# Row variances on one core: the first two loads move ahead of the end of the tile context, everything else behind it

## The chip, the core and the metric

The kernel runs on one core of a Trainium2 chip. The core has five engines with an instruction stream each: TensorE (PE, not used here for computing), VectorE (DVE), ScalarE (ACT), GpSimd (POOL) and SyncE (SP), which here only issues DMA transfers. They meet through semaphores: an instruction can wait until a semaphore has a value and can change one when it is done. Data come from HBM into the core's on-chip memory (SBUF, 128 partitions) over 16 DMA engines. The metric is the device time of one execution in microseconds; the times shown are medians of several.

## The reference

```
def setup_inputs():
    batch, seq, dim = 32, 512, 1024
    return {
        "x": np.random.randn(batch, seq, dim).astype(np.float32),
    }

def reference(x: np.ndarray) -> np.ndarray:
    mean_sq = np.mean(x**2, axis=-1)
    sq_mean = np.mean(x, axis=-1)**2
    return (mean_sq - sq_mean).astype(np.float32)
```

So each of 32 x 512 = 16,384 rows of 1,024 numbers gives one number, its variance. 67.1 MB are read and 64 KB written.

## The kernel before

**Tiling.** The 16,384 rows are spread over 128 partitions, so each partition has 128 rows, called columns here. One column is a tile of 128 x 1,024 numbers. Columns 0 to 95 go through two buffers, `xt0` and `xt1`, of 16 columns (8.4 MB) each, in three turns of two groups (`TURNS`, `NBUF`, `GROUP`). Columns 96 to 127 are the end: loads of 8 and 8 columns back into `xt0`, then 5, 4, 2, 2, 1 and 1 columns and two halves of the last column into `xt_end`, 10 loads in all.

**Who computes.** Of the 16 columns of a group ACT takes six (`NACT`), in batches of three: a pass that sums (`act_mean`, L117), then a pass that squares around the mean and sums (`act_var`, L122). DVE takes ten: two statistics instructions of 512 numbers for each (`halves`, L113) and one that joins them (L216). POOL copies finished variances from `stage` to `mv` (L165) and joins the statistics of eleven end columns (L173 to L192). At the end `END_WHO` says which column is whose; column 126 is ACT's, the halves of column 127 are DVE's.

**Order.** The order of each engine's instructions is written by hand, and so are all waits. SP issues the first two loads at once; the load that refills a buffer waits for `done`, which DVE steps when a group is finished; then the 10 loads of the end; then three stores: columns 0 to 15, the columns up to 120, and the last seven. The last store waits for the last instructions of ACT and DVE (L303, L304). Each load steps its own semaphore (`landed`, `landed_end`) by 16, one for each DMA engine; the stores step `stored`.

**The context.** Tiles and semaphores come from the pools of a tile context (`tc`), and the whole body lies in one `tile_critical` block (L144). What the context adds is no line of the kernel, but it is in the built program: at the entry POOL runs a NOP that steps a semaphore, and every other engine that computes or issues waits for it in a branch; behind the body the engines run a drain each (L144), POOL gathers their semaphores, SP gathers them too, and then come a barrier over all five engines, two instructions of POOL that clear ranges of semaphores, and a second barrier (L308, the end of the context). A barrier here is a drain on each engine, a count that POOL waits for, and a release that POOL gives. Behind all that SP waits until `stored` is 48, that is, until the three stores have landed, and clears that semaphore (L309, L310). One more barrier stands ahead of the body (L325), behind four small constants that POOL writes.

**Place of the code.** Ahead of the body, ACT and DVE each have an alignment (L142): the next instruction of that engine is placed 128 instructions behind a boundary of `FETCH_BLOCK_INSTRUCTIONS`. The loader fills with instructions that are jumped over.

Of the kernel before, what the change touches and what calls it, by code (L numbers as in the profile page):

```python
# [11 lines left out]
def kernel(  # L12
# [14 lines left out]
    nc = tc.nc  # L27
    P = nc.NUM_PARTITIONS
# [6 lines left out]
    N, D = xf.shape  # L35
# [23 lines left out]
    pool = ctx.enter_context(tc.tile_pool(name="pool", bufs=1))  # L59
    xt = [pool.tile([P, GROUP, D], FP32, name=f"xt{b}") for b in range(NBUF)]  # L60
    xt_end = pool.tile([P, ncols - END0 - FIRST, D], FP32, name="xt_end")
    mv = pool.tile([P, 2, ncols], FP32, name="mv")
    stage = pool.tile([P, PER_TURN, 2], FP32, name="stage")
    stats = pool.tile([P, PER_TURN, 2, 6], FP32, name="stats")
    stats_join = pool.tile([P, JOINED, 2, 6], FP32, name="stats_join")
    stats_end = pool.tile([P, ncols - END0, 4, 6], FP32, name="stats_end")
    neg_mean = pool.tile([P, PER_TURN], FP32, name="neg_mean")
    neg_mean_end = pool.tile([P, ncols - END0], FP32, name="neg_mean_end")
    two = pool.tile([P, JOINED, 2], FP32, name="two")
    mu = pool.tile([P, JOINED, 1], FP32, name="mu")  # L70
    dev = pool.tile([P, JOINED, 4], FP32, name="dev")
    psum = ctx.enter_context(tc.tile_pool(name="psum", bufs=1, space=bass.MemoryType.PSUM))
    junk = [pool.tile([P, D], mybir.dt.bfloat16, name=f"junk{i}") for i in range(ACT_BATCH)]
    junk_sq = [psum.tile([P, D], FP32, name=f"junk_sq{i}") for i in range(ACT_BATCH)]

    sync, act, dve, gps = nc.sync, nc.scalar, nc.vector, nc.gpsimd
    landed = [tc.alloc_semaphore(f"landed{b}") for b in range(NBUF)]
    NEND = len(END_LOADS) + len(PIECES)
    landed_end = [tc.alloc_semaphore(f"landed_end{b}") for b in range(NEND)]
    go = tc.alloc_semaphore("go")  # L80
    act_done = tc.alloc_semaphore("act_done")
    done = tc.alloc_semaphore("done")
    copied = tc.alloc_semaphore("copied")
    dve_step = tc.alloc_semaphore("dve_step")
    act_step = tc.alloc_semaphore("act_step")
    gps_step = tc.alloc_semaphore("gps_step")
    stored = nc.alloc_semaphore("stored")

    def load(dst, c0, n, sem, f0=0, f=D):
        b0, pitch, row0 = next(b for b in BLOCKS if b[0] <= c0 < b[0] + b[1])  # L90
        assert c0 + n <= b0 + pitch
        ap = [[pitch * D, P], [D, n], [1, f]] if n > 1 else [[pitch * D, P], [1, f]]
        sync.dma_start(  # L93
            out=dst,
            in_=dataclasses.replace(xf, offset=(row0 + c0 - b0) * D + f0, ap=ap),
        ).then_inc(sem, 16)
# [47 lines left out]
    with tc.tile_critical(sync_engine=ENG.Pool, no_gpsimd_drain=True):  # L144

        for g in range(TURNS * NBUF):
            if g >= NBUF:
                sync.wait_ge(done, g - NBUF + 1)
            load(xt[g % NBUF], g * GROUP, GROUP, landed[g % NBUF])
        sync.wait_ge(done, (TURNS - 1) * NBUF + 1)  # L150
        c = END0
        for b, n in enumerate(END_LOADS):
            k = c - END0
            buf, k = (xt[0], k) if k < FIRST else (xt_end, k - FIRST)
            load(buf[:, k : k + n, :] if n > 1 else buf[:, k, :], c, n, landed_end[b])
            c += n
        f = 0
        for b, n in enumerate(PIECES, len(END_LOADS)):
            load(end_col(c)[:, f : f + n], c, 1, landed_end[b], f, n)
            f += n  # L160

        gps.sem_inc(copied, 1)
        for t in range(TURNS):
            gps.wait_ge(done, (t + 1) * NBUF)
            gps.tensor_copy(  # L165
                out=mv[:, 1, t * PER_TURN : (t + 1) * PER_TURN], in_=stage[:, :, 1]
            ).then_inc(copied, 1)

        part = stats_join.rearrange("p n h (e s) -> p n (h e) s", s=3)
        mean, m2 = part[:, :, :, 1], part[:, :, :, 2]  # L170
        gps.wait_ge(dve_step, 1)
        steps = [
            lambda: gps.tensor_tensor(out=two, in0=mean[:, :, 0:2], in1=mean[:, :, 2:4], op=ALU.add),  # L173
            lambda: gps.tensor_tensor(out=mu, in0=two[:, :, 0:1], in1=two[:, :, 1:2], op=ALU.add),
            lambda: gps.tensor_scalar(out=mu, in0=mu, scalar1=0.25, scalar2=None, op0=ALU.mult),
            lambda: gps.tensor_tensor(out=dev, in0=mean, in1=mu.to_broadcast([P, JOINED, 4]), op=ALU.subtract),
            lambda: gps.tensor_tensor(out=dev, in0=dev, in1=dev, op=ALU.mult),
            lambda: gps.tensor_scalar(out=dev, in0=dev, scalar1=D / 4.0, scalar2=None, op0=ALU.mult),  # L178
            lambda: gps.tensor_tensor(out=dev, in0=dev, in1=m2, op=ALU.add),
            lambda: gps.tensor_tensor(out=two, in0=dev[:, :, 0:2], in1=dev[:, :, 2:4], op=ALU.add),  # L180
            lambda: gps.tensor_tensor(out=mu, in0=two[:, :, 0:1], in1=two[:, :, 1:2], op=ALU.add),
        ]
        k = 0
        runs = []
        for j, c in enumerate(joined):
            if runs and runs[-1][1] + runs[-1][2] == c:
                runs[-1][2] += 1
            else:
                runs.append([j, c, 1])
        for j, c, n in runs:  # L190
            steps.append(
                lambda j=j, c=c, n=n: gps.tensor_scalar(  # L192
                    out=mv[:, 1, c : c + n], in0=mu[:, j : j + n, 0],
                    scalar1=1.0 / D, scalar2=None, op0=ALU.mult,
                )
            )
        for k, step in enumerate(steps):
            if k:
                gps.wait_ge(gps_step, k)
            step().then_inc(gps_step, 1)  # L200
        gps_steps = len(steps)

        with nc.Fori(0, TURNS, engines=[ENG.DVE]):
            take(dve, copied, 1)
            for b in range(NBUF):
                take(dve, landed[b], 16)
                dve.sem_inc(go, 1)
                mine = range(b * GROUP + NACT, (b + 1) * GROUP)
                for j in mine:
                    last = halves(stats[:, j, :, :], xt[b][:, j - b * GROUP, :])  # L210
                last.then_inc(dve_step, 1)
                take(dve, dve_step, 1)
                for j in mine:
                    if j == mine[-1]:
                        take(dve, act_done, 1)
                    last = dve.bn_aggr(out=stage[:, j, :], in_=stats[:, j, :, :])  # L216
                last.then_inc(done, 1)
        n = 0
        waiting = None
        seen = -1  # L220
        for b, c, who in end_cols:
            if who != "D":
                continue
            if b != seen:
                dve.wait_ge(landed_end[b], 16)
                seen = b
            col = end_col(c)
            if c in joined:
                last = halves(stats_join[:, joined.index(c), :, :], col)
                if c == joined[-1]:  # L230
                    last.then_inc(dve_step, 1)
                    n += 1
                continue
            st = stats_end[:, c - END0, :2, :]
            dve.bn_stats(out=st[:, 0, :], in_=col[:, :H])  # L235
            if waiting:
                waiting()
            n += 1
            dve.bn_stats(out=st[:, 1, :], in_=col[:, H:]).then_inc(dve_step, 1)  # L239
            dve_step_of.setdefault(b, n)  # L240

            def waiting(n=n, c=c, st=st):
                dve.wait_ge(dve_step, n)
                return dve.bn_aggr(out=mv[:, :, c], in_=st)  # L244

        c = ncols - 1
        st = stats_end[:, c - END0, : len(PIECES), :]
        f = 0
        for i, size in enumerate(PIECES):
            dve.wait_ge(landed_end[len(END_LOADS) + i], 16)  # L250
            last = dve.bn_stats(out=st[:, i, :], in_=end_col(c)[:, f : f + size])  # L251
            if i == 0:
                waiting()
            f += size
        n += 1
        last.then_inc(dve_step, 1)
        dve.wait_ge(dve_step, n)
        dve.bn_aggr(out=mv[:, :, c], in_=st).then_inc(dve_step, 1)
        dve_steps = n + 1

        act.preload_act_table(ACTF.Square)  # L261
# [15 lines left out]
        for b in range(len(END_LOADS)):  # L277
            mine = [c for bb, c, who in end_cols if bb == b and who == "A"]
            if not mine:
                continue  # L280
# [60 lines left out]
```

## Time and profile before

| what | value |
|---|---|
| time, median of 3 runs | 163.78 us (163.43 to 163.83) |
| time of the profiled execution | 163.64 us |
| its span | 161.9 us |
| what lies around the span | 1.74 us |
| DVE busy | 103.7 us (64%) |
| ACT busy | 106.3 us (66%) |
| POOL busy | 3.6 us (2%) |
| DMA, mean over the span | 415 GB/s |
| first load issued, first group started by DVE | 0.87 us, 23.11 us |
| last ACT pass ends | 160.0 us |

The span runs from the first instruction of the program to the end of its last one, as the profiler recorded them. The time is larger, since it holds work at the start and at the end that belongs to no line of the program. Places in the trace are microseconds from the span's start. Engines are named as above, with a "q" where the instruction is one that only the engine's sequencer runs (waits, drains, branches, DMA issues); those aren't counted as busy. A group of instructions is named by its line in the kernel, its operation, what it writes and reads, and how often it occurs.

### The profile page before, as it was taken

How to read it: one execution, taken by the hardware profiler on the slowest of the kernel's cores; microseconds unless marked ns; L12 is line 12 of the kernel's file. 1: busy time of each engine (PE TensorE's matmuls, PEld its weight loads, DVE VectorE, ACT ScalarE, POOL GpSimd, SP SyncE). 2: the span in 40 equal slices, each digit the busy share in tenths (PEclk: the TensorE clock that was granted, in tenths of full speed). 3: DMA queues.
4: the chain of work that ended last, by engine and by line, in shares of the span. 5: the costliest groups of instructions: out<-in, count | busy, mean ns of one | idle time of the engine just before them, and what ended most of it. 6: DMA issues, size and time to landing. Idle time of an engine off the chain costs nothing. (4 is left out here: it accounts for less than half of the span.)

```text
span 161.9 us, 579 instructions
## 1 busy us (share of the span) xinstructions
DVE 103.7 (64%) x232; ACT 106.3 (66%) x189; POOL 3.6 (2%) x18
## 2 busy tenths in 40 slices
DVE  0000029980599607994099921999039979999994
ACT  3000029990599807996099941999139999799985
POOL 0000000000000000000000000000000000005100
DMA  7969979989988998998997997997989999999991
GB/s 263 518 275 502 518 324 453 518 356 421 518 389 389 518 405 372 518 421 356 518 437 340 518 437 340 518 470 308 518 348 429 421 470 405 400 434 411 423 394 27
DMA packets 2738, 67.19 MB, mean 415 GB/s; under 512 B 688, under 2 KB 688, under 8 KB 1200
## 3 DMA queue, kind: packets, MB, share of 16 engines
q1 hardware_dynamic: 2736, 67.18, 96.7%
q14 instruction: 2, 0.02, 0.1%
HBM read 67.11 MB, written 0.07 MB: 415 GB/s over the span
## 5 line engine op out<-in xcount | busy, mean ns | idle before, releaser
L113 DVE BATCH_NORM_STATS2 stats<-xt 128x6 f32<-128x512 f32 x120 | 71.8, 678 | 49.9 <-DVEq L109 49.9
L117 ACT ACTIVATE junk<-xt 128x1024 bf16<-128x1024 f32 x41 | 42.7, 1042 | 50.4 <-ACTq L109 49.3
L122 ACT ACTIVATE junk_sq<-xt,neg_mean 128x1024 f32<-128x1024 f32 x36 | 39.7, 1104 | 1.5
L113 DVE BATCH_NORM_STATS2 stats_join<-xt 128x6 f32<-128x512 f32 x22 | 13.2, 677 | 0.0
L216 DVE BATCH_NORM_AGGREGATE stage<-stats 128x2 f32<-128x12 f32 x60 | 6.0, 166 | 6.2 <-DVEq L109 5.3
L117 ACT ACTIVATION_READ_ACCUMULATOR junk<-xt 128x1 f32 x41 | 7.6, 186 | 0.0
L122 ACT ACTIVATE junk_sq<-xt_end,neg_mean_end 128x1024 f32<-128x1024 f32 x6 | 6.7, 1111 | 0.1
L122 ACT ACTIVATION_READ_ACCUMULATOR junk_sq<-xt,neg_mean 128x1 f32 x36 | 6.7, 186 | 0.0
L117 ACT ACTIVATE junk<-xt_end 128x1024 bf16<-128x1024 f32 x6 | 6.3, 1046 | 0.4 <-DMA xt_end<-in_x_dram 0.2
L235 DVE BATCH_NORM_STATS2 stats_end<-xt_end 128x6 f32<-128x512 f32 x9 | 6.1, 675 | 0.0
L239 DVE BATCH_NORM_STATS2 stats_end<-xt_end 128x6 f32<-128x512 f32 x9 | 5.8, 642 | 0.0
L122 ACT ACTIVATE junk_sq<-xt,neg_mean_end 128x1024 f32<-128x1024 f32 x5 | 5.5, 1106 | 0.1
L165 POOL COPY mv<-stage 128x32 f32<-128x32 f32 x3 | 0.6, 210 | 133.0 <-DVE stage L216 133.0
L261 ACT ACT_TABLE_LOAD x1 | 1.3, 1283 | 1.3 <-PEq L325 1.3
L244 DVE BATCH_NORM_AGGREGATE mv<-stats_end 128x2 f32<-128x12 f32 x9 | 1.7, 191 | 0.0
L251 DVE BATCH_NORM_STATS2 stats_end<-xt_end 128x6 f32<-128x512 f32 x2 | 1.3, 668 | 0.1
L117 ACT ACTIVATION_READ_ACCUMULATOR junk<-xt_end 128x1 f32 x6 | 1.1, 188 | 0.0
L122 ACT ACTIVATION_READ_ACCUMULATOR junk_sq<-xt_end,neg_mean_end 128x1 f32 x6 | 1.1, 186 | 0.0
L122 ACT ACTIVATION_READ_ACCUMULATOR junk_sq<-xt,neg_mean_end 128x1 f32 x5 | 0.9, 188 | 0.0
L173 POOL TENSOR_TENSOR two<-stats_join 128x22 f32<-128x22 f32 x1 | 0.3, 252 | 12.9 <-DVE stats_join L113 12.9
L192 POOL TENSOR_SCALAR mv<-mu 128x6 f32<-128x6 f32 (+1 forms) x2 | 0.5, 236 | 0.2
L178 POOL TENSOR_SCALAR dev<-dev 128x44 f32<-128x44 f32 x1 | 0.3, 331 | 0.1
(12 smaller groups left out, 2.3 us busy)
## 6 DMA issues: line engine op xcount, KB each, us to landing
xt<-in_x_dram SPq DMA_DIRECT2D x2, 4096.0 KB, 19.5
xt_end<-in_x_dram SPq DMA_DIRECT2D x1, 2560.0 KB, 29.8
xt_end<-in_x_dram SPq DMA_DIRECT2D x1, 2048.0 KB, 34.2
xt_end<-in_x_dram SPq DMA_DIRECT2D x2, 1024.0 KB, 37.1
xt_end<-in_x_dram SPq DMA_DIRECT2D x2, 512.0 KB, 39.3
xt_end<-in_x_dram SPq DMA_DIRECT2D x2, 256.0 KB, 40.0
xt<-in_x_dram SPq DMA_DIRECT2D x6, 24.5
out_dram<-mv SPq DMA_DIRECT2D x1, 52.5 KB, 4.4
```

The costliest lines, as they stand in the source:

```text
L113: last = dve.bn_stats(out=st[:, h, :], in_=xcol[:, h * H : (h + 1) * H])
L117: return act.activation(out=junk[i], in_=xcol, func=ACTF.Copy, scale=-S / D, accum_out=nm)
L122: return act.activation(out=junk_sq[i], in_=xcol, func=ACTF.Square, scale=S, bias=nm, accum_out=var)
L165: gps.tensor_copy(out=mv[:, 1, t * PER_TURN : (t + 1) * PER_TURN], in_=stage[:, :, 1]).then_inc(copied, 1)
L173: lambda: gps.tensor_tensor(out=two, in0=mean[:, :, 0:2], in1=mean[:, :, 2:4], op=ALU.add),
L192: lambda j=j, c=c, n=n: gps.tensor_scalar(out=mv[:, 1, c : c + n], in0=mu[:, j : j + n, 0], scalar1=1.0 / D, scalar2=None, op0=ALU.mult,)
L216: last = dve.bn_aggr(out=stage[:, j, :], in_=stats[:, j, :, :])
L235: dve.bn_stats(out=st[:, 0, :], in_=col[:, :H])
L239: dve.bn_stats(out=st[:, 1, :], in_=col[:, H:]).then_inc(dve_step, 1)
L244: return dve.bn_aggr(out=mv[:, :, c], in_=st)
L251: last = dve.bn_stats(out=st[:, i, :], in_=end_col(c)[:, f : f + size])
L261: act.preload_act_table(ACTF.Square)
```

## The change

Tiles and semaphores no longer come from the context's pools but from the core's own allocators. The `tile_critical` block is gone. Inside the context only three things are left: the two alignments and the first two loads, whose semaphores the context is told not to handle. Then the context is closed, and all else, word for word as it was but one level further out, is written behind it. At the end SP clears the kernel's own semaphores, from `landed0` to `gps_step`, behind the issue of the last store, and then waits for `stored` as before.

In the built program the entry NOP of POOL and the branches that wait for it are gone, and so are the drains, gathers, POOL's two clears and the two barriers behind the body. Two barriers over all five engines, with one more drain on SP, now stand between the first two loads and the rest. DVE's and ACT's instructions are the same in the same order; on both, the four instructions of those two barriers now lie between the alignment and the body.

```
-    pool = ctx.enter_context(tc.tile_pool(name="pool", bufs=1))
-    xt = [pool.tile([P, GROUP, D], FP32, name=f"xt{b}") for b in range(NBUF)]
...
+    def sbuf(name, shape, dtype):
+        return nc.alloc_sbuf_tensor(name, shape, dtype).ap()
+
+    def psum(name, shape, dtype):
+        return nc.alloc_psum_tensor(name, shape, dtype).ap()
+
+    xt = [sbuf(f"xt{b}", [P, GROUP, D], FP32) for b in range(NBUF)]
...
-    landed = [tc.alloc_semaphore(f"landed{b}") for b in range(NBUF)]
+    landed = [nc.alloc_semaphore(f"landed{b}") for b in range(NBUF)]
...
     stored = nc.alloc_semaphore("stored")
+    sems = [*landed, *landed_end, go, act_done, done, copied, dve_step, act_step, gps_step]
...
-        sync.dma_start(
+        return sync.dma_start(
...
     for engine in (act, dve):
         engine.addr_align(FETCH_BLOCK_INSTRUCTIONS, offset=HEAD, max_nops=0)
 
-    with tc.tile_critical(sync_engine=ENG.Pool, no_gpsimd_drain=True):
-
-        for g in range(TURNS * NBUF):
-            if g >= NBUF:
-                sync.wait_ge(done, g - NBUF + 1)
-            load(xt[g % NBUF], g * GROUP, GROUP, landed[g % NBUF])
-        sync.wait_ge(done, (TURNS - 1) * NBUF + 1)
...
+    for g in range(NBUF):
+        dma = load(xt[g], g * GROUP, GROUP, landed[g])
+        tc.no_tile_sem_insts.add(dma.ins.name)
     ctx.close()
     tc.close()
     tc.compile()
+
+    for g in range(NBUF, TURNS * NBUF):
+        sync.wait_ge(done, g - NBUF + 1)
+        load(xt[g % NBUF], g * GROUP, GROUP, landed[g % NBUF])
+    sync.wait_ge(done, (TURNS - 1) * NBUF + 1)
...
+    sync.wait_ge(act_step, act_steps)
+    sync.wait_ge(dve_step, dve_steps)
+    store(early, ncols)
+    sync.sem_clear(range(sems[0].num, sems[-1].num + 1))
     sync.wait_ge(stored, 48)
     sync.sem_clear(stored)
```

## The prediction

> **What bounds the kernel now.** I read the page first, then the windows, then the timeline of the two ends, and last the lines of the program's own synchronization. The page gives span, load queue and last store:
>
> ```profile
> span 161.9 us, 579 instructions
> ...
> q1 hardware_dynamic: 2736, 67.18, 96.7%
> ...
> out_dram<-mv SPq DMA_DIRECT2D x1, 3.5 KB, 1.4
> ```
>
> DVE (64%) and ACT (66%) have room; the 16 DMA engines don't. The windows view (stretch and length, then DVE, ACT and POOL busy, clock, DMA share, GB/s) shows where:
>
> ```profile
> 3.00:22.00 19.00, 0.00 (x0) 0.00 (x0) 0.00 (x0) 1.00 0.96 417
> 22.00:157.00 135.00, 100.92 (x226) 102.12 (x183) 3.40 (x14) 1.00 0.99 428
> ```
>
> From 3 to 157 us it is one unbroken stream of loads, so the end is the start of the stream, plus its length, plus what follows its last bytes. The two ends, by the timeline (start, duration, both us) and by the chain of waits in order of time:
>
> ```profile
> 0.87 0.86 SPq L93 DMA_DIRECT2D xt<-in_x_dram  x2
> 1.30 1.28 ACT L261 ACT_TABLE_LOAD   x1 [1.30 <-PEq L325]
> ...
> 37.13 0.33 SPq L93 DMA_DIRECT2D xt<-in_x_dram  x1
> ```
>
> ```profile
> 117.84 39.74 DMA xt_end<-in_x_dram
> 157.58 0.02 issue
> 157.61 1.16 ACT junk L117 x2
> 158.76 0.02 issue
> 158.79 1.12 ACT junk_sq L122
> ```
>
> The reader is to see three things. The first load is issued at 0.87. The refill of xt0 is issued at 37.13, while the second load lands at 42.27 by its semaphore, so the queue has 5.1 us of work in hand. The end hangs on column 126's load (landed 157.58) and ACT's two passes over it, done at 160.04. The lines of the synchronization (duration ns min/median/max, first and last start):
>
> ```profile
> L325 SPq EVENT_SEMAPHORE  x1: 17/17/17, 0.6 to 0.6; - x1
> ...
> L308 SPq COMPARE_BRANCH  x1: 33/33/33, 0.7 to 0.7; - x1
> ...
> L308 DVEq DRAIN  x2: 19/65/111, 160.0 to 161.5; - x2
> L308 ACTq DRAIN  x2: 8/11/14, 160.1 to 161.1; - x2
> ...
> L310 SPq EVENT_SEMAPHORE_RANGE_CLEAR  x1: 25/25/25, 161.9 to 161.9; - x1
> ```
>
> SP is released from the opening barrier at 0.638, waits in a branch at 0.716 for a POOL NOP (its update is at 0.699), and issues at 0.869. At the other end the last store is issued at 160.055 and its last increment comes at 161.458, yet SP's closing clear starts at 161.868: drains and two barriers of the closed context (L308) stand in between.
>
> **The change part by part.**
>
> *Start.* The branch with its wait for POOL goes; the first load stands right behind SP's release, which ends at 0.655. Between neighbouring SP instructions that wait for nothing the chain shows 0.04 us, so the issue comes at about 0.70 instead of 0.87: 0.17 earlier. Bounds: 0.23 (0.869 less 0.638) and 0, if not the issue sets the first packet. That one starts at 1.890, 1.02 behind the issue; for the last store it is 0.83. I take 0.17, since the whole stream follows its first packet.
>
> *The two barriers moved behind the first loads.* SP now issues a drain and two barriers between the second load and the third; nothing else is queued on SP in between, and the third load waits for `done` until 37.1 anyway. The other engines wait in them for SP (second issue ends about 1.56) and for DVE, whose jump at 0.74 lets it go on at 1.31. Before, two barriers took from 160.76 to 161.87, with two clears in them that go; so they end by 1.6 + 1.1 = 2.7. The work behind them is POOL's `copied`, ACT's table load (1.28, so done near 4) and DVE's first statistics, which all wait for the first load's landing at 23.1. Cost 0 under 19 us of cover; uncovered 1.1. The drain on SP behind two large loads could be thought to wait for them; behind the last store it ran 160.44 to 160.57, before that store's first packet at 160.88, so it doesn't wait for transfers. Were it to, DVE would start 19 us late, and that would be seen at once.
>
> *End.* The tail of the context is gone: drains, NOPs, two barriers, two POOL clears. SP clears the kernel's semaphores behind the third store's issue (0.025 on SP, 0.14 at the longest on POOL) under the store's 1.40 us, and waits for `stored` directly. A waiting sequencer starts 0.017 behind the increment (ACT's last increment 160.038, store 160.055), so the last clear starts at 161.475 instead of 161.868: 0.39 earlier. Bounds 0.33 (another barrier release took 0.08 from increment to record) and 0.41.
>
> *Around the span.* The profiled execution took 163.64, 1.74 more than its span. Behind the span the trace keeps the updates of one semaphore that all engines step in turn: 162.09, 162.12, 162.33, 162.37, 162.40, 162.50, 162.53, 162.57, 162.62, and nine more up to 163.76. The same nine ahead of the span have gaps of 0.02 to 0.11; only here is a gap of 0.21, so one engine came 0.17 late. After the change all but SP have ended by about 159.9, 1.4 us ahead of SP, and can't be late. If SP is one of the later steps (162.40 is the fifth, 0.50 after SP's end, where the first step comes 0.24 after PE's end) the gain is up to 0.28. Bounds -0.1 (a new late step of 0.17 elsewhere, half hidden) to 0.28; 0 if the time doesn't count it. It counts, I think: from the span's start to those last updates are 163.4 to 163.8. I take 0.2.
>
> *Tensors and semaphores from the core instead of the pools.* The built program has them at the same addresses: no instruction more, nothing. Stores, loads and arithmetic are the same, with the same waits.
>
> Sum against the profiled execution: 163.64 - 0.17 - 0.39 - 0.20 = 162.88, so 162.9; span 161.9 - 0.56 = 161.3. The median of the runs, 163.78 (163.43 to 163.83), lies 0.14 above this execution. The range must cover that as well.
>
> *A rule that speaks to the end.* DVE's second closing drain started at 161.52, ACT's and SP's at 161.07: 0.45 late, and POOL had to wait for it. Counting DVE's executed instructions as they lie in the program from the one that the kernel places at its alignment (offset 128), that drain is number 128, counted from 0. After the change four barrier instructions, one move, the loop of 71 and the tail of 52 make 128 in all, numbers 0 to 127: DVE's last statistics stand right ahead of that place.
>
> The Trainium skill, "Runtime: NRT & Kernel Launch", section "Instruction fetch mechanics", says that code is loaded in blocks of 256 instructions ahead of use and that passing from one to the next is mostly hidden. By the page the late drain should cost nothing and the end would gain only from the shorter tail; by the trace the place costs 0.45 when an engine reaches it on the path. My sum is made without either.
>
> **The rivals.**
>
> *1. The work behind the span doesn't follow.* Its steps are set by something else, as code that is loaded there (one 8 KB record of the instruction queue at 162.18, 0.40 long). Then only the ends of the span pay, and of the end perhaps half: 163.64 - 0.17 - 0.20 = 163.27; at worst 163.64 - 0.17 = 163.47. For it: what engines do there isn't recorded. Against: the step that was late belongs to an engine that will be long done.
>
> *2. The change doesn't do what it says:* the first load isn't sooner, because the two 8 KB code records at 1.77 and 1.92, and not the issue, hold its packets, and the clear of the semaphores stands in the way at the end. 163.64 - 0 - 0.33 + 0.14 = 163.45. Against: the first data packet starts at 1.89 on another engine, and the clear has 0.9 us of the store to hide in.
>
> *3. Slower: DVE's tail comes one instruction too long,* because a branch that the program drops now is kept. Then DVE's last aggregate is number 128. At 0.45 it ends at 160.34 instead of 159.89, 0.30 behind ACT's 160.04, and the time is 162.88 + 0.30 = 163.2, still not slower. If the code isn't there and must be loaded, the price is a load record (0.40 to 0.86) plus the 1.02 us from issue to first packet, 1.9 at most: 162.88 + 1.88 - 0.15 = 164.6. It is slower than before from the point where the stall passes 163.78 - 162.88 + 0.15 = 1.05 us. For it: the count ends exactly at the edge. Against: every fall-through branch was dropped before, by the count of DVE's 275 records, and both code loads came at 1.8, long ahead.
>
> **How the numbers follow.** About 0.3%, 0.49 us, is what a measurement of this kernel can tell from no change; faster means below 163.29, slower above 164.27. The forecast has 0.66 and lies at 162.9, with its own bounds of 162.7 (0.23 + 0.41 + 0.28 off) to 163.3 (less of each, and the runs' 0.14). Rival 1 has 0.14, rival 2 0.10, rival 3 and what else could lengthen the path 0.10, of which some stays within 0.3%. Faster: 0.66 and a little of rival 1, 0.69. Same: the rest of rivals 1 and 2, and rival 3 at its low price, 0.23. Slower: 0.08. The range, 162.5 to 163.5, holds the forecast with the runs' scatter of 0.2 and the first two rivals.
>
> **What would show it.** In the changed profile: first issue near 0.70 and the first packet near 1.72; ACT's first pass over xt at 22.98 instead of 23.15; ACT's last pass done near 159.87; the last store's landing 1.40 behind its issue, with SP's last clear within 0.05 of it; span 161.3. The prediction is wrong if the first load lands no sooner, if a DVE or ACT instruction near the end starts late without a data wait, if SP's drain behind the first loads lasts, or if the time falls by less than the span.

## The result, and the profile after

The changed kernel takes 164.17 us (median of 8 runs, 164.04 to 164.29) against 163.68 of the kernel before beside it (8 runs, 163.43 to 163.83). The ratio is 1.0025, with a 95% interval of 1.0016 to 1.0035: a little slower, where the forecast was 162.9 with a range of 162.5 to 163.5. The profiled execution took 164.04, with a span of 162.73; before it was 163.64 and 161.89. So the span grew by 0.83 us, what lies around it shrank by 0.43 (from 1.74 to 1.31), and the time rose by 0.40. The forecast had the span 0.56 shorter, so inside the span 1.39 us are to be explained.

The page of the changed kernel:

```profile
span 162.7 us, 561 instructions
...
q1 hardware_dynamic: 2736, 67.18, 96.5%
q14 instruction: 3, 0.02, 0.1%
```

Eighteen instructions fewer, the same packets of loads and stores, and three records of the queue that brings code (q14). Its timeline at the start (start, duration, engine, line) and the lines of its own synchronization (duration ns min/median/max, first and last start):

```profile
0.72 0.86 SPq L98 DMA_DIRECT2D xt<-in_x_dram  x2
2.37 1.28 ACT L270 ACT_TABLE_LOAD   x1 [2.37 <-PEq L154]
```

```profile
L154 SPq DRAIN  x3: 7/7/128, 1.6 to 2.0; - x3
...
L154 DVEq DRAIN  x2: 10/36/63, 1.3 to 2.1; - x2
...
L154 SPq EVENT_SEMAPHORE  x2: 17/17/17, 2.0 to 2.3; - x2
```

The first load is issued at 0.72 instead of 0.87. The two barriers behind the first loads (L154) end at 2.3, SP's drain among them lasts 0.128, and ACT's table load follows at 2.37. None of it holds up anything: DVE and ACT wait for the first landing until 23.

The other end is read from the chain of waits in order of time:

```profile
118.15 40.66 DMA xt_end<-in_x_dram
158.81 0.02 issue
158.84 1.16 ACT junk L122 x2
159.99 0.02 issue
160.02 1.24 ACT junk_sq L127 x2
```

It is the same chain as before, column 126's load and ACT's two passes. But that load has landed at 158.81 instead of 157.58, 1.23 us later, though it was issued only 0.31 later and its queue was never empty. From there on the change does what it should: ACT's passes end 2.44 after the landing, as before, the last store lands at 162.684 (1.40 behind its issue, as before), and the closing clear starts 0.016 behind that, where it was 0.41 behind.

So the time went into the load stream. Each load steps its semaphore 16 times, which is read here as one step for each of the 16 DMA engines (the stretch from 158.5 to 159.9 us below fits that). The trace keeps each step, but not which engine made it:

| us | before: first / 15th / 16th step | after: first / 15th / 16th step |
|---|---|---|
| first load | 22.15 / 22.75 / 22.89 | 21.99 / 22.77 / 23.14 |
| sixth load of the end (columns 123, 124) | 154.30 / 154.90 / 155.02 | 154.14 / 154.93 / 155.31 |
| column 126's load | 156.87 / 157.47 / 157.58 | 156.70 / 157.49 / 158.81 |

In the changed kernel the first of the 16 is 0.16 sooner all the way down, as forecast. But the fifteenth isn't sooner at all, and the eighth of the first load comes at 22.53 instead of 22.32: the engines' first packets, 64 KB each, take 2.5 to 3.7 us here (2.4 to 3.2 before), so part of the gain was lost on other engines too. The last is 0.37 behind the fifteenth from the first load on (before 0.14), and 1.33 behind it at the end (before 0.11). A load has landed when its last step is made, so the slowest engine sets the time. From the sixth load of the end to column 126's, the eighth, the last step moves 3.505 us, against 2.566 before: 0.94 are lost there and 0.29 had been lost before.

The view of the DMA engines from 155 to 158 us shows what is in between. In the kernel before, the whole stretch belongs to loads and stores:

```profile
DMA packets 599, 1.17 MB, mean 389 GB/s; under 512 B 199, under 2 KB 199, under 8 KB 599
...
q1 hardware_dynamic: 599, 1.17, 103.2%
```

In the changed kernel one packet of code is among them:

```profile
DMA packets 525, 1.16 MB, mean 386 GB/s; under 512 B 135, under 2 KB 135, under 8 KB 524
...
q1 hardware_dynamic: 524, 1.15, 100.6%
q14 instruction: 1, 0.01, 0.7%
```

It starts at 155.93. Two 4,096 B packets right behind it, at 156.25 and 156.75, take 0.50 and 0.48 us, where such a packet takes 0.16. The same view from 158 to 162 us (busy tenths of all 16 engines and GB/s, in slices of 0.1 us) of the changed kernel shows the lonely engine:

```profile
DMA  8865400010001000000000000000000000000000
GB/s 236 274 113 126 117 25 20 20 41 21 20 20 41 20 20 20 9 21 8 0 0 0 0 0 0 0 0 0 0 0 0 0 0 0 0 0 0 0 0 0
```

From 158.5 to 159.9 the core moves some 20 GB/s, a sixteenth or so of the 386 it moved before: that is what is to be expected if fifteen engines are done and one still has its share of three loads and a store.

The three code records in or behind each kernel's span (8,192 B each) start at 1.77, 1.92 and 162.18 before, and at 2.00, 4.92 and 155.93 after. Before, the first two are ahead of or level with the first data packet (1.89), and the third is behind the last store. After, the first data packet comes at 1.73, ahead of them all, and the third record is in the stream. The second one, at 4.92, shows its price as well: a 64 KB packet that starts at 5.22, where the record ends, takes 2.95 us, where such packets take 2.42 later on. That gave the theory for the experiments: *two code loads now fall into a stream that has no gap, each sets one DMA engine back, and the stream never catches up.* The rivals: the stream is longer because of the moved barriers or the place of DVE's and ACT's loops, or the difference is only in when the first load is issued.

### The profile page after: what moved, and what is told of

It reads as the page before. It is cut to its first block, busy times and chain, and to the rows that moved or that the text cites. A ratio compares the mean times of both kernels' runs of the same rounds, so it can differ in the third digit from the quotient of the medians.

```text
span 162.7 us, 561 instructions
## 1 busy us (share of the span) xinstructions
DVE 103.8 (64%) x232; ACT 106.3 (65%) x189; POOL 3.6 (2%) x18
```

## The experiments

Ten kernels were run, all beside the kernel before. "Alignment" is the place of the first instruction behind the jump, 128 in both kernels of this case; "number" counts the engine's instructions from there. The time of the kernel before was 163.57 beside the first four (16 runs), 163.60 beside the next four (19 runs) and 163.60 beside the last two (9 runs); it was 163.68 beside the changed kernel, so a tenth between times of different sets says nothing.

### DVE's code at 64

```
-    for engine in (act, dve):
-        engine.addr_align(FETCH_BLOCK_INSTRUCTIONS, offset=HEAD, max_nops=0)
+    act.addr_align(FETCH_BLOCK_INSTRUCTIONS, offset=HEAD, max_nops=0)
+    dve.addr_align(FETCH_BLOCK_INSTRUCTIONS, offset=64, max_nops=0)
```

> The changed kernel with DVE's code placed 64 instructions behind the boundary instead of 128; nothing else. Theory A: the code record at 155.93 in the changed kernel is DVE's, whose sequencer runs some ten instructions ahead of its engine, reaches the end of its code block (DVE's kernel code ends exactly there) and loads the next block into the saturated stream; one of the 16 DMA engines then falls about 0.95 us further behind. With 64 instructions more room the record is gone from the stream, column 126's load lands near 157.9 instead of 158.81, the span is 161.8 and the time 163.2. Rival B: the record belongs to an engine that has ended early (POOL, SP): unchanged, 164.1 to 164.2. Rival C: not a code record but the second store at 155.2 holds that DMA engine: also unchanged.

Measured: 164.57 (164.45 to 164.73), ratio 1.0060 [1.0043, 1.0076]. The record at 155.9 is gone, so it was DVE's. The time is still worse, since other records have come: there are four, at 1.73, 1.76, 7.90 and 59.52, all in or at the start of the stream, and the last step of the first load comes 1.03 behind the fifteenth. By the count DVE's loop (numbers 5 to 75) now lies across number 64, which would be an edge if there is one every 128 instructions; that would account for the two late records, but no run tests it. Behind the record at 59.52 the last step of a landing is 2.02 behind the fifteenth, and later only 0.6; that engine didn't catch up (its steps stay 1.8 behind those of the kernel before), the others fell back. The start shows a second thing, in the lines of the synchronization of this kernel:

```profile
L154 DVEq DRAIN  x2: 10/37/64, 3.9 to 4.2; - x2
```

DVE's first drain starts at 3.9 instead of 1.3: DVE stood still for 2.6 us right behind its jump (ACT did so in the next run, where its place is changed: 3.60 instead of 1.15). No line names what it waited for; by its place it would be the code that it jumped to, which isn't shown. Here it lies under the first load.

### ACT's code at 64

```
-    for engine in (act, dve):
-        engine.addr_align(FETCH_BLOCK_INSTRUCTIONS, offset=HEAD, max_nops=0)
+    act.addr_align(FETCH_BLOCK_INSTRUCTIONS, offset=64, max_nops=0)
+    dve.addr_align(FETCH_BLOCK_INSTRUCTIONS, offset=HEAD, max_nops=0)
```

> The changed kernel with ACT's code placed 64 instead of 128 instructions behind the boundary; DVE as it was. Theory A: the record at 155.9 stays, column 126 lands near 158.8, time 164.1 to 164.2. If instead ACT loads that block (its code ends near number 105 from the alignment), the record goes and the time falls to 163.2. The two code records at 2.0 and 4.9 stay if ACT's jump to its aligned place still enters another block.

Measured: 164.08 (164.00 to 164.39), 1.0033 [1.0021, 1.0046]. The record at the end stays (156.04), as it must if it is DVE's. Two more come, at 7.56 and 135.17, which go with ACT's changed place. ACT's place isn't the cause, and moving it brings nothing. But it shows that the price of records doesn't simply add up: with two more in the stream, column 126 lands at 158.91, only 0.10 behind the changed kernel. The records at 135.17 and 156.04 cost the landing 0.52 and 0.43. In this kernel two engines are already late by then (the fifteenth step of the first load is 0.38 behind the fourteenth), and a landing waits for the slowest alone; which engine carries a record the trace doesn't keep.

### An entry wait inside the context

```
+    entry = nc.alloc_semaphore("entry")
...
+    gps.sem_inc(entry, 1)
+    sync.wait_ge(entry, 1)
     for g in range(NBUF):
         dma = load(xt[g], g * GROUP, GROUP, landed[g])
```

> The changed kernel with one thing put back: ahead of the first load SP waits for a step of POOL, as before the change. First issue about 0.85 instead of 0.72. Theory S: at the start two code records of 8 KB are asked for at about 0.75 and reach the DMA engines at 1.77 and later; with the first load issued 0.15 sooner its packets are there first, one DMA engine serves them in between, and that engine is 0.25 to 0.4 us late from the first load on. With the wait back the records come first again: the first load has wholly landed at 22.9 instead of 23.14, all landings are 0.25 sooner, time 163.9. Rival: the late DMA engine at the start has nothing to do with the order of records and packets; the stream starts 0.15 later still, first load landed at 23.3, time 164.3.

Measured: 164.20 (163.98 to 164.44), 1.0037 [1.0020, 1.0054]. The edit missed its aim: in the built program the wait came to stand on the second load, and the first was issued at 0.720 as before. So it tells nothing of the start, but it is a second sample of the changed kernel's order: records at 2.06, 4.83 and 155.85, the last engine 0.53 behind the fifteenth at the first load and 1.53 behind it at column 126.

### DVE's code at 160

```
-    for engine in (act, dve):
-        engine.addr_align(FETCH_BLOCK_INSTRUCTIONS, offset=HEAD, max_nops=0)
+    act.addr_align(FETCH_BLOCK_INSTRUCTIONS, offset=HEAD, max_nops=0)
+    dve.addr_align(FETCH_BLOCK_INSTRUCTIONS, offset=160, max_nops=0)
```

> The changed kernel with DVE's code placed 160 instead of 128 instructions behind the boundary, so the end of the block is reached 32 instructions sooner in DVE's tail, at about 140 to 147 us. Theory A: a code record comes there instead of at 155.9; from then on one DMA engine is 0.5 to 1.0 us behind the others in every landing to the end, since the stream has no gap in which it could catch up; time 163.9 to 164.3. Rivals B and C: the record at 155.9 stays where it was, the landings before it are as in the changed kernel, time 164.1 to 164.2.

Measured: 164.09 (163.93 to 164.40), 1.0032 [1.0022, 1.0042]. The edge now lies 32 instructions sooner in DVE's code, at number 96, and the record moves with it, from 155.9 to 138.9. The view of the DMA engines of this kernel from 138 to 140 us:

```profile
q1 hardware_dynamic: 48, 0.80, 95.1%
q14 instruction: 1, 0.01, 1.0%
```

From the first to the second load of the end the last step now moves 10.73 us, against 9.72 in the changed kernel: 1.01 lost here. From the sixth to the eighth it moves 2.525, as in the kernel before: nothing lost there any more. The same price, 17 us sooner, and kept to the end (158.89 for column 126, against 158.81). That is the theory's main point: when the record comes doesn't matter, so long as it comes into the stream.

### DVE held back from the edge

```
     for i, size in enumerate(PIECES):
-        dve.wait_ge(landed_end[len(END_LOADS) + i], 16)
+        if i == 0:
+            take(dve, landed_end[len(END_LOADS)], 16)
+        else:
+            dve.wait_ge(landed_end[len(END_LOADS) + i], 16)
```

`take` is a wait that DVE's sequencer runs as an instruction of its own; nothing behind it is looked at until the first half of column 127 has landed. `wait_ge` puts the wait on the statistics instruction, and the sequencer goes on ahead of it.

> The changed kernel with one more instruction on DVE: the wait for the first half of column 127 takes the semaphore down as well, which makes it an instruction of DVE's sequencer that nothing behind it can overtake. Theory A (DVE's sequencer runs ahead past the end of its code block and loads the next block into the stream): the sequencer is held until 158.2, the code record moves from 155.9 to 159 or later, where no load is left; column 126 lands near 157.9 instead of 158.81, span about 161.8, time 163.2. Rival B (the block is loaded whenever the engine comes near, or by another engine): the record stays at 155.9, time 164.1 to 164.2 or a little more.

Measured: 163.37 (163.21 to 163.52), 0.9980 [0.9971, 0.9990]. DVE's code is one instruction longer, so it does cross the edge now, and yet the time is 0.8 us below that of the changed kernel. The DMA engines of this kernel from 155 to 158 us have loads and a store only, and from 158 to 162 the code:

```profile
q1 hardware_dynamic: 510, 1.17, 101.9%
```

```profile
q1 hardware_dynamic: 413, 0.11, 12.2%
q14 instruction: 1, 0.01, 0.5%
```

The record starts at 160.23, behind the last load, and from the sixth to the eighth load of the end the last step moves 2.57 again. The store isn't the cause either: it is issued here at 155.59, into the same stretch as in the changed kernel (155.17), and nothing is lost. The end of DVE's timeline shows one thing more:

```profile
159.76 0.64 DVE L263 BATCH_NORM_STATS2 stats_end<-xt_end 128x6 f32<-128x512 f32 x1
160.44 0.21 DVE L270 BATCH_NORM_AGGREGATE mv<-stats_end 128x2 f32<-128x12 f32 x1
```

The last aggregate is number 128, the one behind the edge. It starts at 160.44, 0.03 behind the statistics before it, while the record runs from 160.23 to 160.56: DVE doesn't stand still at the edge. What is left is the start: records at 1.98 and 5.28, behind the first data packet at 1.73, and the last engine 0.93 behind the fifteenth at the first load.

### The first load later again

Ahead of the tile context, so that it stands ahead of the first load:

```
+    entry = nc.alloc_semaphore("entry")
+    nc.gpsimd.sem_inc(entry, 1)
+    nc.sync.wait_ge(entry, 1)
+    nc.sync.sem_inc(entry, -1)
+    nc.sync.sem_inc(entry, 1)
+    nc.sync.wait_ge(entry, 1)
+    nc.sync.sem_inc(entry, -1)
```

> The changed kernel with the first load held back by about 0.2 us (SP steps and waits for a semaphore of its own and one of POOL's ahead of it; the wait of the earlier run had come to stand on the second load). First issue about 0.93. Theory S (at the start two code records ride behind the first packets on one DMA engine): records at about 1.77 and 1.92 again, ahead of the data; the last DMA engine of the first load is 0.1 behind the one before it instead of 0.37 to 0.53, the first load has landed at 22.9 to 23.0 instead of 23.14, later landings follow, and the time is 163.8 to 164.0 although the start is later. Rival: the late DMA engine doesn't depend on the order; first load landed at 23.35, time 164.35.

Measured: 163.76 (163.50 to 163.97), 1.0007 [0.9996, 1.0018]. In its timeline the first load is issued 0.20 us later than in the changed kernel, and the time is 0.4 us less than that one's:

```profile
0.92 0.86 SPq L98 DMA_DIRECT2D xt<-in_x_dram  x2
```

Why, shows in the view of the DMA engines from 1 to 6 us (GB/s in slices of 0.125 us; an 8 KB record alone in a slice makes 66). First the changed kernel, then this one:

```profile
GB/s 0 0 0 0 0 1049 3146 2097 66 1049 0 524 0 0 0 524 0 0 0 0 0 0 0 0 0 0 0 0 0 524 0 1638 0 2097 1049 2621 524 0 0 0
```

```profile
GB/s 0 0 0 0 0 0 66 2687 1573 1573 1573 0 0 524 0 524 0 0 0 0 0 0 0 0 0 0 0 0 0 0 0 524 2097 1049 3146 524 1049 0 0 0
```

In the changed kernel the 66 stands behind three slices of data; here it stands ahead of the first, at 1.76, with the second record at 1.91 just ahead of the first data packet at 1.93. The last engine is then 0.09 behind the fifteenth at the first load, and still 0.11 behind it at the sixth load of the end. The record at the end (155.66) is there as before, and costs 1.00: from the sixth to the eighth load takes 3.57.

### Both

> Both edits together. Theories A and S: neither code record is in the stream, column 126 lands at about 157.6 to 157.7 as before the change, the tail is the changed kernel's shorter one: span about 161.5, time 162.9, faster than before by 0.7. If only A holds: 163.4. If only S: 163.9. If neither: 164.4.

Measured: 162.73 (162.65 to 162.74), 0.9944 [0.9927, 0.9960], 0.87 us below the kernel before. Records at 1.76, 1.91 and 159.46: none in the stream. The page of this kernel and its chain of waits:

```profile
span 161.4 us, 566 instructions
...
q14 instruction: 3, 0.02, 0.1%
```

```profile
117.79 39.70 DMA xt_end<-in_x_dram
157.49 0.02 issue
157.51 1.16 ACT junk L122 x2
158.67 0.02 issue
158.70 1.24 ACT junk_sq L127 x2
```

There are three code records here too; only their places differ. Column 126 has landed at 157.49, 0.03 behind the fifteenth step, and all that the change was to gain behind the stream is there.

### The kernel before with DVE's code at 160

```
-    for engine in (act, dve):
-        engine.addr_align(FETCH_BLOCK_INSTRUCTIONS, offset=HEAD, max_nops=0)
+    act.addr_align(FETCH_BLOCK_INSTRUCTIONS, offset=HEAD, max_nops=0)
+    dve.addr_align(FETCH_BLOCK_INSTRUCTIONS, offset=160, max_nops=0)
```

> The kernel before the change with DVE's code placed 160 instead of 128 instructions behind the boundary; nothing else. Theory A: the end of the block is reached in DVE's tail near 138 us, a code record comes there, one DMA engine is 0.8 to 1.0 us behind the others from then on, column 126 lands near 158.5 instead of 157.58 and the time is 164.4 to 164.7 although no other line is changed. Rival: what costs the changed kernel its time is something else in it; here 163.6.

Measured: 164.61 (164.23 to 164.84), 1.0052 [1.0033, 1.0072]. That is 1.0 us over the kernel before, with none of the change made. The record at 162.18 is gone, so that one was DVE's too; it now comes at 138.92. Its DMA engines from 138 to 140 us:

```profile
q1 hardware_dynamic: 53, 0.84, 100.0%
q14 instruction: 1, 0.01, 1.0%
```

From the first to the second load of the end its last step moves 10.74 us, against 9.71 in the kernel before: 1.02 lost to the record. In the profiled execution, the slowest of the four (164.84), there is a second loss: the first two records start at 1.93 and 2.08, behind the first data packet at 1.88, although the load is issued at 0.87 as in the kernel before. Two engines are late from there on, and the first load lands at 23.23 instead of 22.89. So its column 126 lands 1.29 later (158.87); whether the other three, at 164.23 to 164.76, lost at the start too isn't shown.

### How late the first load has to be

Both edits, with shorter delays ahead of the first load: one instruction on SP, then two.

```
+    entry = nc.alloc_semaphore("entry")
+    nc.gpsimd.sem_inc(entry, 1)
+    nc.sync.wait_ge(entry, 1)
+    nc.sync.sem_inc(entry, -1)
```

> The version that held DVE's sequencer and delayed the first load to 0.92, now with one SP instruction fewer ahead of the load: issue at about 0.79, first packet near 1.80, between the places of the two code records (1.76 and 1.90). Theory S: the record at 1.90 falls behind the first packets; if both share the late DMA engine, the last engine of the first load is again 0.3 to 0.9 behind the one before it and the time is 163.0 to 163.4; if the first record alone does the harm, 162.6. Rival: a later start costs what it is late and nothing else; here 162.6, since it starts 0.13 sooner than at 0.92 (162.73).

```
+    entry = nc.alloc_semaphore("entry")
+    nc.sync.sem_inc(entry, 1)
+    nc.sync.sem_inc(entry, -1)
```

> The same with two SP instructions ahead of the first load: issue at about 0.86, as before the change (0.87), first packet near 1.88, at the second record's place. Theory S: as in the kernel before the records come in time, the last engine is about 0.1 behind the one before it, and the time is 162.6 to 162.8. Should the order be lost by a hair, 163.0 to 163.4. Rival as above: 162.7.

Measured: with the issue at 0.79 the six executions fall into two groups, 163.27 to 163.37 and 162.79 to 162.83, median 163.05, ratio 0.9957 [0.9938, 0.9976]. The profiled one is of the first group, with records at 2.27 and 5.20 and the last engine 0.82 behind the fifteenth. With the issue at 0.85 all four take 162.79 to 162.96, median 162.90, 0.9954 [0.9937, 0.9970]: records at 1.77 and 1.94, the first data packet at 1.85. So with DVE held an issue at 0.85 was late enough in all four executions, by their times, and at 0.79 in half of the six. Neither shorter delay gives a version shown to be better than the 0.92 one. Nor is 0.85 a bound that holds everywhere: the kernel before with DVE at 160 issues at 0.87, and in its profiled execution the records lost the race. The 19 runs of the kernel before in that set lie at 163.38 to 163.69 and, five of them, at 163.90 to 164.09, which would fit such a race there too; no profile of one of the five was kept. The start, by the profiled executions:

| kernel | first issue | first data packet | first two records | 16th step behind 15th, first load |
|---|---|---|---|---|
| before | 0.87 | 1.89 | 1.77, 1.92 | 0.14 |
| after | 0.72 | 1.73 | 2.00, 4.92 | 0.37 |
| DVE held | 0.72 | 1.73 | 1.98, 5.28 | 0.93 |
| held, issue 0.79 | 0.79 | 1.81 | 2.27, 5.20 | 0.82 |
| held, issue 0.85 | 0.85 | 1.85 | 1.77, 1.94 | 0.19 |
| first load later | 0.92 | 1.93 | 1.76, 1.91 | 0.09 |
| both | 0.92 | 1.93 | 1.76, 1.91 | 0.03 |
| before, DVE at 160 | 0.87 | 1.88 | 1.93, 2.08 | 0.15 |

The last column hides it when two engines are late: in the last row the fifteenth step is itself 0.39 behind the fourteenth.

## Why the prediction was wrong, step by step

**"I take 0.17, since the whole stream follows its first packet": this step failed.** The issue came 0.15 sooner and the first packet 0.16 sooner, and the first of the 16 engines stayed 0.16 ahead to the end. But the stream ends with its last engine, not with its first packet. The sooner issue put the first data ahead of the two code records, and the engine that had to fit them in was late from the first load on: by the sixth load of the end the landing was 0.29 later instead of 0.17 sooner. That is 0.46 of the missing 1.39. One of the prediction's own signs of being wrong, a first load that lands no sooner, had come (23.14 instead of 22.89). The prediction had these records in hand. Rival 2 thought that they might hold the packets, and dismissed it because "the first data packet starts at 1.89 on another engine". Its question was whether the code delays the data's first packet; what counted is which of the two comes first on the engine that carries both.

**"DVE's last statistics stand right ahead of that place", and "My sum is made without either": the second step that failed.** The place was right, and rival 3 was built on it: "the count ends exactly at the edge". But the rival asked for one instruction too many and a DVE that stands still. Neither was needed. DVE's code ends at number 127, and a record is fetched all the same, while DVE is still at its statistics; DVE waits for nothing because of it, as its groups in the waits of the changed kernel show, which name transfers alone near the end:

```profile
DVE stats_end L260 <- DMA xt_end<-in_x_dram: 0.5, 1, 0.5
DVE stats_end L244 <- DMA xt_end<-in_x_dram: 0.3, 1, 0.3
```

The price of 0.45 that rival 3 took for an instruction behind the edge doesn't show either: with DVE held, number 128 starts without a pause. In the kernel before the drain there was late because of the place (with DVE at 160 it comes 0.11 behind the wait ahead of it, instead of 0.53), but not because it needed that record: it ran at 161.52, and the record started at 162.18. So the record goes with the crossing and brings something further on; what, isn't shown. The loser is the load stream: 0.94 us, the rest of the 1.39. Before, the drains of the closed context stood between DVE's last statistics and the edge, and held the sequencer until its work was done; so the record came at 162.18. The change took these drains away and so let the sequencer run on. That this is the mechanism, and not the place alone, is shown by the run with DVE held back: longer code, the edge crossed, no loss.

The Trainium skill, "Runtime: NRT & Kernel Launch", section "Instruction fetch mechanics", says that passing to the next block is mostly hidden. For the engine whose code it is, the changed kernel agrees: DVE started nothing late for it. For the loads it isn't hidden: one record in this stream cost them 0.94 to 1.02 us (less only with ACT at 64, as said there).

**The barriers behind the first loads: right.** They end at 2.3 (2.7 was worked out), SP's drain takes 0.128 and doesn't wait for transfers, and nothing waits for them.

**The end: right.** 0.39 was forecast; the closing clear stands 0.016 behind the last landing instead of 0.41, which is 0.39. SP's clear of the other semaphores takes 0.064 under the store.

**Around the span: right in kind, too small.** Forecast 0.20, bounds -0.1 to 0.28; measured 0.43. Four engines step the closing semaphore at 2.58, 161.37, 161.41 and 161.45, far ahead of SP. SP is the fifth, as supposed. Its step comes 0.125 behind its end instead of 0.504, which is 0.38 of the gain, and what follows takes 1.31 instead of 1.37. The upper bound took 0.24, PE's distance from its end to its step, for the least that SP's could be (0.50 less 0.24 is 0.26, not quite the 0.28 given); it can be 0.125. Rival 1, that this wouldn't follow, is out.

**The sum, mended.** Start +0.29 instead of -0.17, record at the end +0.94, the tail from landing to span's end -0.40 (0.39 of it at the closing clear), around the span -0.43: together +0.40, which is 164.04 against 163.64. With both records out of the stream the same terms give, from the kernel with both edits, -0.09 for the landing of column 126, -0.39 for the tail and -0.43 around the span: 162.73, its measured time.

Held alone, the median falls by 0.80 from the changed kernel's 164.17, delayed alone by 0.41, both by 1.44. The two parts together are thus the whole of the loss. That they don't add up to the last tenth isn't followed further; the start's price differs between executions (0.37 to 0.93 in the table above). The second load's landing before, which the prediction gives as 42.27, is 42.21 by its sixteenth step; nothing rests on that.

Left open: which DMA engine carries the code, since the trace doesn't keep it, what the record brings, and why two 4 KB packets behind the record, and not only the record's own 0.34 us, are slow. Together the record (0.34) and what the two packets take over 0.16 (0.34 and 0.32) make about 1.0 us, the measured price; that they ran on one engine is inferred from their times. A start that keeps the sooner issue and needs no code record (a body without jumps to an aligned place) wasn't tried.

## What to carry to other kernels

Where a kernel is one unbroken stream of loads, look at the last of the 16 landing steps and its distance from those before it, not at GB/s (from the fifteenth alone is not enough, since two engines can be late): an engine that was set back once stayed back here, and a code record in the stream cost about 1 us where it fell on the engine that ended last. Count where each engine's code crosses from one block to the next, and keep something that holds its sequencer (a wait of its own, a drain) ahead of a crossing that would fall into the stream; removing synchronization from the end of a program can let the code load move forward. And issuing the first load sooner is no gain by itself if it overtakes the code that the other engines are fetching at that moment.

## What the runs showed of the hardware

- One 8 KB code record in the stream cost 0.94 to 1.02 us of landing time (changed kernel, DVE at 160, kernel before with DVE at 160, first load later), though the record itself takes 0.33 to 0.34. With ACT at 64, where two engines were late already, two records cost 0.52 and 0.43. At the start, with the queues still empty, two records cost nothing that shows if they come ahead of the first data packet or level with it (last engine 0.03 to 0.19 behind).
- A record that comes behind the first data packets, of 64 KB each, can be held up: the second record starts at 4.83 to 5.28 in six kernels (the changed one, ACT at 64, entry wait, DVE at 160, DVE held with the issue at 0.72 and 0.79), where the first data packets start at 1.73 to 1.81 and take some 3 us. It isn't always: 2.08 in the kernel before with DVE at 160, with the first packet at 1.88. The Trainium skill, "DMA: Bandwidth & Descriptors", section "Queues, rings and completion order", says that each DMA engine takes turns between its queues a whole packet at a time; these starts fit that.
- DVE's sequencer runs well ahead of the engine: the record that goes with the edge ahead of number 128 starts at 155.93, when DVE itself has just started number 118 (at 155.90). At the start of the kernel before, the two records start 1.05 and 1.17 us behind the jumps of ACT and DVE, in that order; subtracted here, that would be 154.8 to 154.9, with DVE at number 115 (an estimate from these two times). With the sequencer held, in four kernels, the record starts 1.27 to 1.29 us behind the start of the wait that held it.
- Behind the program, SP's closing step comes 0.125 us after its end if the other engines are long done, and 0.504 if they end along with it.
